# First layer's weighted expert rows: through a table in memory, or by products with the one-hot

## The chip, the cores and the metric

The kernel runs on one core of one Trainium2 chip. The metric is the time of one execution in microseconds of device time, lower is better. A core has a matrix engine (TensorE, PE in the profile; its weight loads are PEld), VectorE (DVE), ScalarE (ACT), GpSimd (POOL) and SyncE (SP), and 16 DMA engines that serve the queues of all of them.

## What is computed

Two layers of a diffusion backbone over 256 latent and 256 context tokens of width 1024. Each layer has four mixers (gated recurrence, short convolution, retention, attention), an output projection and a mixture of experts. In the first layer the experts serve all 512 tokens, in the second only the 256 latent ones. The part that matters here:

```python
def hierarchical_moe(h, w_rg, b_rg, w_re, b_re, w_gate, w_up, w_down):
    # top-1 of 4 expert groups, then top-2 of the 4 experts in it
    ...
    combine = jnp.sum(one_hot(expert_id, N_EXPERTS) * weights[..., None], axis=1)
    y = jnp.zeros(h.shape, jnp.float32)
    for e in range(N_EXPERTS):                       # 16 experts
        hidden = silu(h @ w_gate[e]) * (h @ w_up[e]) # 1024 -> 512
        y = y + combine[:, e:e + 1] * (hidden @ w_down[e])
    return y
...
x = x + mod_x[5] * y[latent];  ctx = ctx + mod_c[5] * y[context]
```

So every token gets the weighted sum of two expert rows, and that sum goes to the residual X, times a gate per column.

## The kernel before

X is kept transposed: for each of 8 column blocks j a tile of 128 columns (partitions) by 256 tokens, for latent and context tokens (`X(j, s)`).

The experts are worked through by token slots. Every expert has 64 or 96 slots, in blocks of 32; a *round* is 128 slots, four blocks. The first layer has 10 rounds (`rounds`, from `BLOCKS[0] = (2, 3, 3, 2)`), the second has 8. A round that holds two experts uses two column groups of 64 in TensorE; one that has blocks of three slots to an expert uses four of 32. All expert products are in float32.

For the first layer, the code traces each round r as follows (loop in `moe`): `gate_up(r)` multiplies the slots' rows with the gate and up weights (tiles `g` and `u`) and forms `hs`; `fetch(r + 2)` computes slots and weights of a later round and issues the gather of its rows from the memory copy `hd` on POOL's queue; `place(r + 1)` transposes the gathered rows (`gx`); `turned(hs)` transposes the hidden values (`hT`); `down(r, hT)` multiplies with the down weights (`d`, two PSUM buffers).

Expert weights arrive in tiles of 1 MB on SP's queue, in the order of use, as many in flight as `keep(LIVE[l][...])` says. All large tiles, weights, gathered rows and outputs, share 22 slabs (`NSLAB`). One-hots and hidden values share the six tiles of tag "t".

What becomes of a round's output differs. In rounds 0 to 7 of the first layer (`r < by_dma`) `down` scales it by the slot's weight, half on ACT and half on VectorE, and an indirect DMA on POOL's queue writes the rows to a table `ys` in memory, with two rows for every token; the row number is computed in `weigh` (lines from 1368 on), from a fourth plane of `mw_` that tells first from second expert. The table was filled with zeros earlier, in the first layer's mixers (line 992). After round 7, `collect` reads the table back, adds the two rows of each token and, in round 9, transposes them (32 transposes, line 1525) and adds them to X.

Rounds 8 and 9, and all rounds of the second layer, go the other way: `down` splits the weighted output into a high and a low float32r half (`ohl`, VectorE and ACT), `mark` writes a one-hot of the round's slots by tokens (`P`), and `scatter` multiplies both halves with it: per column block j, two rounds by two halves are 4 products (tile `sct`, 512 columns in the first layer, 256 in the second), which VectorE then adds to X times the gate (line 1501, two instructions in the first layer). `scatter` is a generator; one step is one column block. Its PSUM buffers are named by tags: `TGS = (("a",), ("a", "pj"))` for the two layers, while the last pair gets `TG[1]`, "pj" with three buffers. There is one buffer "a".

The order of instructions on each engine is made when the kernel is built: earlier traced ones first, a later one moved up where an earlier one is expected to wait. `tc.issue_after(x)` keeps instructions behind x.

Of the kernel before, what the change touches and what calls it, by code (L numbers as in the profile page):

```python
# [63 lines left out]
SF = ('pf', 1, 7)  # L64
NTT = 6

LIVE = [[5, 6, 4, 7, 14, 14, 15, 11, 8], [5, 5, 8, 11, 15, 18, 12]]

SPLIT = [['VG', 'VV', 'VG', 'VG', 'VG', 'VG', 'VG', 'VG', 'VV', 'VG', 'VG', 'VG', 'VG', 'VG'], ['VG', 'VG', 'VG', 'VG', 'VG', 'VG', 'VG', 'VG', 'VG', 'VG', 'VG', 'VG', 'VG', 'GV']]

# [45 lines left out]
def build(tc, xT, cT, vec, cst, ada, w_in, w_out, wg, wu, wd, outT, es, dbg=None):  # L116
# [20 lines left out]
    def ps(tag, shape=(512,), name="ps"):  # L137
        return psp.tile([128] + list(shape), F32, name=nm(name), tag=tag, bufs=PSB[tag])
# [18 lines left out]
    def tt(out, a, b, op, eng=V):  # L157
        return eng.tensor_tensor(out, a, b, op=op)  # L158
# [305 lines left out]
    def mixers(l, X, sums, first, fill, deep):  # L464
# [522 lines left out]
                pre[g] = split_w(take('in', l, g), ENG[l][g])  # L987
        weave((chain(hgrn_out(), att_norm()), MW[l][2]), (chain(ret_v(), conv()), MW[l][3]), (decays(), MW[l][4]), (fill(1), MW[l][5]))
        keep(deep[1])
        if full:  # L990
            zero = wt([512], "t")
            G.memset(zero, 0.0)
            for i in range(4):
                nc.scalar.dma_start(ys[256 * i:256 * i + 256].rearrange("(p a) (b f) -> p (a b) f", a=2, b=2),
                                    zero[:, None, :].to_broadcast([128, 4, 512]))
        for g in PST[l][1]:
            if g not in pre:
                pre[g] = split_w(take('in', l, g), ENG[l][g])
# [115 lines left out]

    keep_ = [con.tile([128, 4, 16], F32, name=k) for k in ("posm", "ovc")]
    mb_ = con.tile([128, 4, 16], BF16, name="mb")
    mw_ = con.tile([128, 4, 4, 16], BF16, name="mw")

    ys = drm.tile([2 * NT + 128, 1024], F32, name="ys")

    def moe(l, X, sums, gate, filler):
        n = NT if l == 0 else NX
# [200 lines left out]
        if sorted_:  # L1323
            by_load(comb16)

        mw = mw_[:, :nch, 0:3]
        NP = 3
        if not direct:

            NP = 4  # L1330
            r16, f16 = e_.rearrange("p c g e -> p c (g e)"), rest.rearrange("p c g e -> p c (g e)")
            V.tensor_scalar(rest, sets(rank)[:, :, 1:5], 1.0, None, op0=OP.is_equal)
            tt(rest, rest, mb4, OP.mult)
            if sorted_:
                by_load(f16)
            V.tensor_copy(mw_[:, :nch, 3], f16)
        V.tensor_copy(mw[:, :, 0], comb16)
        tt(rest16, comb16, mw[:, :, 0], OP.subtract)
        V.tensor_copy(mw[:, :, 1], rest16)
# [8 lines left out]
        V.tensor_copy(flag, pf[0:1, 0:1])  # L1348
        NR = len(rounds)

        by_dma, ysl, yrow, behind = 0 if direct else NR - 2, {}, [], [None]

        def weigh(q, Sq):

            nb = nbs[q]
            for r_ in range(nb):
                p = ps("m", [NP, 4], name="ww")
                for c in range(nch):
                    mm(p, Sq[:, c, 128 * r_:128 * r_ + 128], mw_[:, c, 0:NP, 4 * q:4 * q + 4], c == 0, c == nch - 1)
                w = wt([1], "wsl", bufs=6)  # L1360
                jk = wt([4, 4], "wslj", bufs=2)
                eo = C_EXP + (0 if nb == 3 else 12) + 4 * r_
                tt(jk[:, 0:NP], p, late(eo, 4)[:, None, :].to_broadcast([128, NP, 4]), OP.mult)
                V.tensor_reduce(w, jk[:, 0:3], axis=AX.XY, op=OP.add)
                ws[base[q] + r_] = w
                if base[q] + r_ < by_dma:

                    fx = idxf[base[q] + r_]
                    y, yi = wt([3], "ysl", bufs=2), wt([1], "ysi", I32, bufs=6)
                    V.tensor_reduce(y[:, 0:1], jk[:, 3], axis=AX.X, op=OP.add)  # L1370
                    V.tensor_scalar(y[:, 1:2], late(C_TOK + 1, 1), float(2 * NT + 256), None, op0=OP.add)
                    V.scalar_tensor_tensor(y[:, 1:2], fx, 0.0, y[:, 1:2], op0=OP.is_lt, op1=OP.mult)
                    V.scalar_tensor_tensor(y[:, 2:3], fx, 2.0, y[:, 0:1], op0=OP.mult, op1=OP.add)
                    tt(yi, y[:, 1:2], y[:, 2:3], OP.add)
                    ysl[base[q] + r_] = yi

        def fetch(r):
            q, i = rounds[r]
# [13 lines left out]
        def place(r):  # L1392

            if direct:
                S = wt([nch * 128], "t").rearrange("p (c s) -> p c s", c=nch)
                slot_of(S.rearrange("p c (e s) -> p c e s", e=2), 2 * r, 2, cap0)
                x = rowt[(r + 1) // 2][:, r % 2].rearrange("p (j s) -> p j s", j=8)
            else:
                row = rowt.pop(r)
                x = row[:, 1].rearrange("p (j s) -> p j s", j=8)  # L1400
                rv = row[:, 0].rearrange("p (j f) -> p j f", j=8)
            for hf in range(2):
                p = ps(TG[2][hf], [4, 128], name="gx")
                for j in range(4):
                    if direct:
                        for c in range(nch):
                            mm(p[:, j], hrow[c].rearrange("p (j f) -> p j f", j=8)[:, 4 * hf + j], S[:, c], c == 0, c == nch - 1)
                    else:
                        T.transpose(p[:, j], rv[:, 4 * hf + j], ident)
                if hf:  # L1410
                    act(x[:, 4:8], p)
                else:
                    V.tensor_copy(x[:, 0:4], p)  # L1413
            Xg[r] = x
            if r >= by_dma:
                mark(r)

        def experts(r):
            q, i = rounds[r]
# [35 lines left out]
        def turned(hs):  # L1455
            p = ps(TG[3], name="hT")
            for jj in range(4):
                behind[0] = T.transpose(p[:, 128 * jj:128 * jj + 128], hs.rearrange("p (f e) -> p f e", e=4)[:, :, jj], ident)
            hT = wt([512], "t").rearrange("p (a b) -> p a b", a=4)
            act(hT, p.rearrange("p (a b) -> p a b", a=4))  # L1460
            return hT

        def down(r, hT):
            pd = [ps("h", name="d") for _ in range(2)]
            for jj in range(4):
                if jj == 2:
                    finish(r, 4)
                for nn in range(2):
                    for b, m, e in columns(r):
                        mm(pd[nn][b:b + m], hT[:, jj, b:b + m], W[e][4 + jj // 2][:, jj % 2, 512 * nn:512 * nn + 512],  # L1470
                           jj == 0, jj == 3)
            finish(r, 5)
            w = ws.pop(r)
            if r < by_dma:
                if r % 2 == 0:
                    yrow.append(sl([2, 1024], name="y"))
                o = yrow[-1][:, r % 2]
                act(o[:, 0:512], pd[0], AF.Copy, scale=w)
                V.tensor_scalar(o[:, 512:1024], pd[1], w, None, op0=OP.mult)
                nc.gpsimd.indirect_dma_start(out=ys[:, :], out_offset=bass.IndirectOffsetOnAxis(ap=ysl.pop(r), axis=0),  # L1480
                                             in_=o, in_offset=None)
                return
            ohl = sl([2, 1024], F32R, "o")
            for nn in range(2):
                fs = slice(512 * nn, 512 * nn + 512)
                act(ohl[:, 0, fs], pd[nn], AF.Copy, scale=w)
                V.scalar_tensor_tensor(ohl[:, 1, fs], pd[nn], w, ohl[:, 0, fs].bitcast(F32),  # L1487
                                       op0=OP.mult, op1=OP.subtract)
            outs[r] = ohl
# [17 lines left out]
                        outs.pop(r), Pm.pop(r)  # L1507
                yield

        def collect(tags=None):  # L1510

            tags = tags or TGS[l]
            yt = []
            for c in range(nch):
                y = sl([2, 1024], name="y")
                nc.gpsimd.dma_start(y, ys[256 * c:256 * c + 256].rearrange("(p a) f -> p a f", a=2))
                yt.append(y)
            yield
            for c in range(nch):
                tt(yt[c][:, 0], yt[c][:, 0], yt[c][:, 1], OP.add, (V, G)[c % 2])  # L1520
            for j in range(8):
                p = ps(tags[j % len(tags)], name="sct")
                for c in range(nch):
                    with tc.issue_after(behind[0].ins):
                        T.transpose(p[:, 128 * c:128 * c + 128], yt[c][:, 0, 128 * j:128 * j + 128], ident)
                for s in range(ns):
                    V.scalar_tensor_tensor(X(j, s), p[:, NX * s:NX * s + NX], gate[:, j, s:s + 1], X(j, s),
                                           op0=OP.mult, op1=OP.add)
                yield

        fetch(0)
        fetch(1)
        if not by_dma:
            mark(0)
        pend, sc = [], iter(())
        for r in range(NR):
            if r >= NR - 2 and l + 1 < DEPTH:
# [5 lines left out]
                fetch(r + 2)  # L1543
            if r + 1 < NR:
                place(r + 1)
            if by_dma:
                hs = turned(hs)
                if r == NR - 1:
                    run(sc)
            else:  # L1550
                for _ in range(SCJ[l]):
                    next(sc, None)
                hs = turned(hs)
            down(r, hs)
            if r < by_dma:
                if r == by_dma - 1:
                    sc = collect(TG[1] + TGS[l])
                    next(sc)
                continue
            pend.append(r)  # L1560
            if len(pend) == 2 and r < NR - 1:
                run(sc)
# [202 lines left out]
```

## Time and profile before

| | us |
|---|---|
| median of 3 runs | 1180.85 |
| lowest, highest | 1178.14, 1181.89 |
| profiled execution, its own time | 1176.74 |
| its span, first to last instruction | 1175.0 |

| engine | busy, us | share |
|---|---|---|
| PE | 1092.7 | 93% |
| PEld | 688.1 | 59% |
| DVE | 512.1 | 44% |
| ACT | 370.3 | 32% |
| POOL | 218.8 | 19% |

The profile is that of one execution. Engines run side by side and wait for each other by semaphores. The share of busy time is a mean over stages that differ, so the profile is read for the stage that the change touches: the first layer's experts, from about 395 to 670 us, where 96 weight tiles of 1 MB stream in. In the rows further on, "idle before" in brackets is the time an engine stood still before an instruction, and the arrow names what ended it.

### The profile page before, as it was taken

What the parts mean: (1) busy time and instruction counts of PE and PEld (TensorE: products, weight loads), DVE (VectorE), ACT (ScalarE), POOL (GpSimd) and SP (SyncE); (2) the same over time, 40 slices, a digit from 0 to 9 for tenths busy, and PEclk for the clock granted to TensorE, in tenths of its full rate; (3) what the DMA queues carried; (4) which work ended last, traced back from release to release, by engine and by line L of the source; (5) the groups of instructions that cost most, each with busy time, mean ns of one, the idle gap of its engine ahead of it and who ended that gap; (6) DMA issues with size and microseconds to landing.
All of it is one profiled execution on the core that took longest, in us unless ns stands there. A gap on an engine that the chain in (4) does not pass through costs nothing. (4 is left out here: it accounts for less than half of the span.)

```text
span 1175.0 us, 16520 instructions
## 1 busy us (share of the span) xinstructions
PE 1092.7 (93%) x6577; PEld 688.1 (59%) x6577; DVE 512.1 (44%) x1000; ACT 370.3 (32%) x628; POOL 218.8 (19%) x168
## 2 busy tenths in 40 slices
PE   5999989999999989999898889999899799999997
PEld 2699876674576453333233459867767644565653
DVE  1647576656663810101001574686876421212122
ACT  5544357533442101001010454347754211101010
POOL 0235270410131001000012323353203200000000
PEclk9999999999999999999999989999999899999999
DMA  9812105765437999999799942472255889899991
GB/s 385 327 66 68 41 1 215 261 238 218 172 120 273 416 421 422 420 421 422 306 390 409 379 180 85 178 275 73 102 185 179 323 323 420 359 423 420 422 388 37
DMA packets 48548, 316.18 MB, mean 269 GB/s; under 512 B 5712, under 2 KB 7376, under 8 KB 12112
## 3 DMA queue, kind: packets, MB, share of 16 engines
q1 hardware_dynamic: 42320, 295.52, 63.4%
q0 software_dynamic: 3024, 13.11, 2.7%
q10 hardware_dynamic: 3120, 6.41, 1.5%
q8 instruction: 55, 0.90, 0.3%
q14 instruction: 29, 0.24, 0.1%
HBM read 303.49 MB, written 11.53 MB: 268 GB/s over the span
## 5 line engine op out<-in xcount | busy, mean ns | idle before, releaser
L152 PE MATMUL pf<-hxh,wsp 128*128 128x512 f32 (+1 forms) x640 | 178.9, 363 | 11.0 <-ACT hxh L155 5.0
L152 PE MATMUL g<-w,row 128*64 128x512 f32 (+1 forms) x704 | 148.0, 598 | 2.3 <-DVE row L1413 2.1
L152 PE MATMUL u<-w,row 128*64 128x512 f32 (+1 forms) x704 | 142.6, 593 | 1.3 <-DMA w<-in_wu_dram 1.3
L158 POOL TENSOR_TENSOR wsp<-w,wsp 128x1024 fp32r<-128x1024 f32 x34 | 94.2, 2774 | 250.9 <-ACT wsp L155 204.9
L152 PE MATMUL d<-w,t 128*64 128x512 f32 (+1 forms) x704 | 133.3, 597 | 1.5 <-ACT t L155 1.4
L152 PEld LDWEIGHTS pf<-hxh,wsp 128*128 128x128 f32 x640 | 114.5, 191 | 34.4 <-ACT hxh L155 7.1
L152 PE MATMUL pf<-hxl,wsp 128*128 128x512 f32 (+1 forms) x320 | 114.7, 360 | 2.2 <-POOL hxl L158 2.0
L158 DVE TENSOR_TENSOR t<-t,u 128x512 f32<-128x512 f32 x18 | 12.4, 687 | 232.6 <-PE u L152 232.6
L152 PEld LDWEIGHTS u<-w,row 128*64 128x64 f32 (+1 forms) x704 | 55.3, 127 | 74.9 <-issue 69.5
L152 PEld LDWEIGHTS g<-w,row 128*64 128x64 f32 (+1 forms) x704 | 52.7, 127 | 76.2 <-issue 68.6
L152 PEld LDWEIGHTS d<-w,t 128*64 128x64 f32 (+1 forms) x704 | 48.0, 128 | 78.5 <-issue 67.7
L152 PE MATMUL ptk<-wsp,hxh 128*128 128x256 f32 x480 | 90.3, 287 | 0.0
L155 ACT ACTIVATE wsp<-w 128x1024 fp32r<-128x1024 f32 x72 | 73.7, 1053 | 13.9 <-PE pf L152 7.7
L152 PEld LDWEIGHTS ptk<-wsp,hxh 128*128 128x128 f32 x480 | 75.2, 191 | 2.3 <-issue 1.2
L152 PE MATMUL pw<-mixh,wsp 128*128 128x512 f32 (+1 forms) x256 | 68.5, 352 | 2.2 <-POOL wsp L158 1.3
L158 POOL TENSOR_TENSOR K<-K,F 64x512 f32<-64x512 f32 (+1 forms) x46 | 58.6, 1273 | 59.4 <-issue 24.1
L152 PEld LDWEIGHTS pf<-hxl,wsp 128*128 128x128 f32 x320 | 61.5, 192 | 12.7 <-POOL hxl L158 3.4
L152 PE MATMUL ptk<-wsp,hxl 128*128 128x256 f32 x240 | 68.2, 284 | 0.0
L158 DVE TENSOR_TENSOR wsp<-w,wsp 128x1024 fp32r<-128x1024 f32 x38 | 52.3, 1377 | 31.2 <-ACT wsp L155 31.1
L158 DVE TENSOR_TENSOR Q<-Q,F 64x256 f32<-64x256 f32 (+3 forms) x60 | 55.8, 935 | 22.8 <-PE sc L152 19.5
L155 ACT ACTIVATE row<-gx 128x512 f32<-128x512 f32 x18 | 10.8, 598 | 163.7 <-PE gx L152 88.6
L155 ACT ACTIVATE t<-g 128x512 f32<-128x512 f32 x18 | 10.7, 597 | 162.6 <-PE g L152 162.6
(281 smaller groups left out, 1562.5 us busy)
## 6 DMA issues: line engine op xcount, KB each, us to landing
w<-in_wg_dram SPq DMA_DIRECT2D x64, 1024.0 KB, 10.5
w<-in_wu_dram SPq DMA_DIRECT2D x64, 1024.0 KB, 12.1
w<-in_wd_dram SPq DMA_DIRECT2D x64, 1024.0 KB, 16.1
w<-in_ada_dram SPq DMA_DIRECT2D x48, 1024.0 KB, 6.7
w<-in_w_in_dram SPq DMA_DIRECT2D x28, 1024.0 KB, 7.9
w<-in_w_out_dram SPq DMA_DIRECT2D x8, 1024.0 KB, 6.1
X<-in_xT_dram SPq DMA_DIRECT2D x4, 1024.0 KB, 5.1
ys<-t ACTq DMA_DIRECT2D x4, 1024.0 KB, 5.9
```

The source lines that it names most:

```text
L152: return T.matmul(out, lhsT, rhs, start=start, stop=stop, **kw)
L155: return S.activation(out, in_, f, **kw)
L158: return eng.tensor_tensor(out, a, b, op=op)
```

## The change

The table `ys`, its zero fill, the row numbers in `weigh`, the fourth plane of `mw_`, the indirect writes and `collect` go. All ten rounds of the first layer end as rounds 8 and 9 did: high and low half, one-hot, and products, always for two rounds together. The steps of a pair's `scatter` are traced in the rounds after it: `SCJ[0] = 6` column blocks in the next round, between `place` and `turned`, and the last two in the round after that. The last pair (8, 9) stays where it was. The weight tiles in flight from round 1 on go from 15 to 13, and from round 8 on from 11 to 12. The second layer's code stays as it is.

```diff
-LIVE = [[5, 6, 4, 7, 14, 14, 15, 11, 8], [5, 5, 8, 11, 15, 18, 12]]
+LIVE = [[5, 6, 4, 7, 14, 14, 13, 12, 8], [5, 5, 8, 11, 15, 18, 12]]
...
-        if full:
-            zero = wt([512], "t")
-            G.memset(zero, 0.0)
-            for i in range(4):
-                nc.scalar.dma_start(ys[256 * i:256 * i + 256].rearrange("(p a) (b f) -> p (a b) f", a=2, b=2),
-                                    zero[:, None, :].to_broadcast([128, 4, 512]))
...
-    mw_ = con.tile([128, 4, 4, 16], BF16, name="mw")
-
-    ys = drm.tile([2 * NT + 128, 1024], F32, name="ys")
+    mw_ = con.tile([128, 4, 3, 16], BF16, name="mw")
...
-        mw = mw_[:, :nch, 0:3]
-        NP = 3
-        if not direct:
-
-            NP = 4
-            r16, f16 = e_.rearrange("p c g e -> p c (g e)"), rest.rearrange("p c g e -> p c (g e)")
-            V.tensor_scalar(rest, sets(rank)[:, :, 1:5], 1.0, None, op0=OP.is_equal)
-            tt(rest, rest, mb4, OP.mult)
-            if sorted_:
-                by_load(f16)
-            V.tensor_copy(mw_[:, :nch, 3], f16)
+        mw = mw_[:, :nch]
...
-                if base[q] + r_ < by_dma:
-
-                    fx = idxf[base[q] + r_]
-                    y, yi = wt([3], "ysl", bufs=2), wt([1], "ysi", I32, bufs=6)
...
-                    ysl[base[q] + r_] = yi
...
-            if r >= by_dma:
-                mark(r)
+            mark(r)
...
-            if r < by_dma:
-                if r % 2 == 0:
-                    yrow.append(sl([2, 1024], name="y"))
-                o = yrow[-1][:, r % 2]
-                act(o[:, 0:512], pd[0], AF.Copy, scale=w)
-                V.tensor_scalar(o[:, 512:1024], pd[1], w, None, op0=OP.mult)
-                nc.gpsimd.indirect_dma_start(out=ys[:, :], out_offset=bass.IndirectOffsetOnAxis(ap=ysl.pop(r), axis=0),
-                                             in_=o, in_offset=None)
-                return
...
-        def collect(tags=None):
...
-            if by_dma:
-                hs = turned(hs)
-                if r == NR - 1:
-                    run(sc)
-            else:
-                for _ in range(SCJ[l]):
-                    next(sc, None)
-                hs = turned(hs)
-            down(r, hs)
-            if r < by_dma:
-                if r == by_dma - 1:
-                    sc = collect(TG[1] + TGS[l])
-                    next(sc)
-                continue
+            for _ in range(SCJ[l]):
+                next(sc, None)
+            down(r, turned(hs))
             pend.append(r)
             if len(pend) == 2 and r < NR - 1:
                 run(sc)
```

## Rows read from the trace of the kernel before

**Rows 1.** Busy time in stretches: length, busy us (instructions), PEclk, DMA share, GB/s.

```profile
core 0: us, PE busy (x) PEld busy (x) DVE busy (x) ACT busy (x) POOL busy (x), PEclk, DMA share, GB/s
400.00:500.00 100.00, 92.84 (x554) 39.14 (x552) 19.88 (x87) 9.01 (x15) 7.00 (x7) 0.97 1.01 421
500.00:600.00 100.00, 95.14 (x704) 32.55 (x704) 9.43 (x21) 9.70 (x16) 7.79 (x8) 0.98 0.95 385
...
570.00:580.00 10.00, 9.65 (x40) 3.41 (x40) 1.08 (x2) 1.20 (x2) 0.00 (x0) 0.83 0.42 143
220.00:230.00 10.00, 10.00 (x51) 7.42 (x50) 4.18 (x5) 7.07 (x13) 1.27 (x4) 1.00 0.84 307
```

**Rows 2.** PE in order of time: start, us, instruction, rounds 4 and 8.

```profile
517.01 1.07 PE L1409 MATMUL gx<-cb,row 128*128 128x128 f32 x8
518.48 0.75 PE L1458 MATMUL hT<-cb,t 128*128 128x128 f32 x4 [0.40 <-DVE row L1413]
...
519.98 7.09 PE L152 MATMUL d<-w,t 128*32 128x512 f32 x64
...
622.42 7.09 PE L152 MATMUL d<-w,t 128*64 128x512 f32 x32 [0.75 <-ACT t L155]
```

**Rows 3.** PE's waits from 390 to 672 us: total us, times, longest.

```profile
PE gx L1409 <- DMA row<-hd,ixi: 6.4, 2, 3.3
PE hT L1458 <- DVE row L1413: 3.3, 8, 0.4
PE ww L152 <- DVE ixa L1289: 1.5, 2, 1.1
PE d L152 <- ACT t L155: 1.4, 2, 0.7
PE u L152 <- DMA w<-in_wu_dram: 1.3, 1, 1.3
PE sct L152 <- DVE X L1501: 0.9, 1, 0.9
PE hT L1458 <- DVE t L158: 0.8, 1, 0.8
```

**Rows 4.** Groups by shape, 390 to 672 us: count, busy us, mean ns, idle before.

```profile
L152 PE MATMUL sct<-t,o 128*128 128x512 f32 x32 | 8.2, 403 | 0.9 <-DVE X L1501 0.9
...
L1525 PE MATMUL sct<-cb,y 128*128 128x128 f32 x32 | 4.3, 278 | 0.0
```

**Rows 5.** PE in order of time, round 9: collect's transposes and the down products.

```profile
647.01 2.35 PE L1525 MATMUL sct<-cb,y 128*128 128x128 f32 x20
649.29 1.93 PE L152 MATMUL d<-w,t 128*64 128x512 f32 x6
651.15 0.66 PE L1525 MATMUL sct<-cb,y 128*128 128x128 f32 x4
...
660.22 3.07 PE L152 MATMUL sct<-t,o 128*128 128x512 f32 x12
```

**Rows 6.** PE in order of time, round 6.

```profile
569.76 1.09 PE L1409 MATMUL gx<-cb,row 128*128 128x128 f32 x8 [3.06 <-DMA row<-hd,ixi]
...
574.00 7.51 PE L152 MATMUL d<-w,t 128*64 128x512 f32 x32
```

**Rows 7.** POOL in order of time, around rounds 5 and 6.

```profile
557.70 0.98 POOL L1480 DMA_INDIRECT ys<-y,ysi  x1 [9.19 <-DMA ys<-y,ysi]
558.98 0.98 POOL L1301 DMA_INDIRECT row<-hd,ixi  x1 [0.30 <-DMA w<-in_wd_dram]
```

**Rows 8.** POOL in order of time, the first gather.

```profile
404.41 1.16 POOL L1301 DMA_INDIRECT row<-hd,ixi  x1 [22.99 <-DVE mw L1341]
```

**Rows 9.** DVE in order of time, additions of the last pair of products.

```profile
663.14 4.01 DVE L1501 SCALAR_TENSOR_TENSOR X<-sct,mods,X 128x256 f32<-128x256 f32 x10
```

**Rows 10.** The page's DMA queues: packets, MB, share of 16 engines.

```profile
q0 software_dynamic: 3024, 13.11, 2.7%
```

**Rows 11.** PE in order of time, second layer's round 2.

```profile
1015.56 0.74 PE L152 MATMUL sct<-t,o 128*128 128x256 f32 x4 [0.58 <-DVE X L1501]
```

More of the change, by code (lines that the diff above doesn't have):

```diff
@@ L1349, in moe @@
         NR = len(rounds)
-        by_dma, ysl, yrow, behind = 0 if direct else NR - 2, {}, [], [None]
         def weigh(q, Sq):
@@ L1356, in weigh @@
             for r_ in range(nb):
-                p = ps("m", [NP, 4], name="ww")
+                p = ps("m", [3, 4], name="ww")
                 for c in range(nch):
-                    mm(p, Sq[:, c, 128 * r_:128 * r_ + 128], mw_[:, c, 0:NP, 4 * q:4 * q + 4], c == 0, c == nch - 1)
+                    mm(p, Sq[:, c, 128 * r_:128 * r_ + 128], mw_[:, c, :, 4 * q:4 * q + 4], c == 0, c == nch - 1)
                 w = wt([1], "wsl", bufs=6)
-                jk = wt([4, 4], "wslj", bufs=2)
+                jk = wt([3, 4], "wslj", bufs=2)
                 eo = C_EXP + (0 if nb == 3 else 12) + 4 * r_
-                tt(jk[:, 0:NP], p, late(eo, 4)[:, None, :].to_broadcast([128, NP, 4]), OP.mult)
-                V.tensor_reduce(w, jk[:, 0:3], axis=AX.XY, op=OP.add)
+                tt(jk, p, late(eo, 4)[:, None, :].to_broadcast([128, 3, 4]), OP.mult)
+                V.tensor_reduce(w, jk, axis=AX.XY, op=OP.add)
                 ws[base[q] + r_] = w
-                if base[q] + r_ < by_dma:
-                    fx = idxf[base[q] + r_]
-                    y, yi = wt([3], "ysl", bufs=2), wt([1], "ysi", I32, bufs=6)
[L1370 to L1374, printed above, removed]
-                    ysl[base[q] + r_] = yi
         def fetch(r):
@@ L1457, in turned @@
             for jj in range(4):
-                behind[0] = T.transpose(p[:, 128 * jj:128 * jj + 128], hs.rearrange("p (f e) -> p f e", e=4)[:, :, jj], ident)
+                T.transpose(p[:, 128 * jj:128 * jj + 128], hs.rearrange("p (f e) -> p f e", e=4)[:, :, jj], ident)
             hT = wt([512], "t").rearrange("p (a b) -> p a b", a=4)
@@ L1508, in scatter @@
                 yield
-        def collect(tags=None):
[L1512 to L1529, printed above, removed]
         fetch(0)
         fetch(1)
-        if not by_dma:
-            mark(0)
+        mark(0)
         pend, sc = [], iter(())
```

## The prediction

> **What bounds the kernel now.** The views were read in this order: busy time in stretches, the order of TensorE's instructions in one round, TensorE's waits in the expert stage, and then the rows of the operations that come and go.
>
> The change works on the first layer's expert stage, about 395 to 670 us. There two resources are nearly full at once [rows 1]: the DMA engines are at a share of 1.01 and 421 GB/s, and PE is busy for 92.8 and 95.1 us of two stretches of 100. Which of them sets the pace? The reader is to look at 570 to 580 us: the DMA share falls to 0.42 (143 GB/s) while PE is busy for 9.65 of 10 us. The transfers had run ahead and were waiting for buffers, and PE went on. [Rows 2] say the same from PE's side: the down products of a round take 7.09 us at 520 us, as 64 narrow ones, and 7.09 us at 622 us, as 32 of twice the width. A step waiting for data would not repeat to the hundredth. And [rows 3]: of PE's waits from 390 to 672 us only 1.3 us are for a weight transfer (a row of 0.2 us more is not shown); all its waits make 16.0 us, with 0.4 us in two rows that are not shown. So PE sets the pace, the DMA engines run close behind, and what is added on PE costs its own time less what it fills of those 16 us.
>
> **The change, part by part.**
>
> *Products added.* Rounds 0 to 7, which went to the table, now form four pairs, each of 8 column blocks x 2 rounds x 2 halves (high and low part) = 32 products of 512 columns. Before has exactly one such pair, rounds 8 and 9: 32 products, busy 8.2 us [rows 4], that is 0.256 us each. Four pairs: 4 x 8.2 = **+32.8 us**.
>
> *What it costs to put them between others.* In before the pair runs at the end, in runs of up to 12. The new ones run inside rounds, and layer 0's tag list has one PSUM buffer for them ("a"): block j+1 waits until VectorE has added block j to X. The last round shows what the instruction order does with such waits: the transposes of the collected rows stand ahead of the down products in the code, and in the trace one bank's 4 transposes alternate with 6 and more down products [rows 5]. So a block goes into the down products whenever its buffer is free. That breaks column groups which otherwise run side by side: 6 down products took 651.15 - 649.29 = 1.86 us, where 7.09 / 32 x 6 = 1.33 us is the undisturbed pace [rows 2, 5]. Over the whole step: 660.22 - 647.01 = 13.2 us, less 7.1 for the down products and 4.3 for the transposes [rows 4], leaves 1.8 us for three breaks, 0.6 us each. Per pair I count five breaks: of the six blocks issued in the even round one fills the wait before the hidden transposes (hT), one the wait for their copy, four fall into the down products; of the two in the odd round one breaks something. 4 x 5 x 0.6 = **+12.0 us**. The lower end is 0 (all blocks in waits or at group edges). The upper end is the case that they don't interleave, rival B.
>
> The Trainium skill, "TensorEngine Tiling (Array Packing)", section Key Properties, states that changing the tiling mode drains TensorE, and these breaks go from column tiles to the full array and back. By that rule the term cannot be nothing; without it the sum below would be 12.0 us smaller. The 1.8 us for three breaks agree with it.
>
> *Collect removed.* In round 9 the time from the first transpose to the first product of the last pair is 13.2 us, in which the down products need 7.1 us and the wait for the copy of hT about 0.9 (0.7 as the wait for it in [rows 3], and 0.2 on the way). The rest, **-5.3 us**, goes. The reads of the table and the two additions on POOL lay beside.
>
> *Waits that go, or are filled.* (1) Round 6's place step waited 3.06 us for its gathered rows [rows 6]. The gather was issued at 558.98, behind a table write that itself stood 9.19 us on POOL's queue until the previous table write had landed [rows 7]. With no table write there, the gather no longer stands behind it. PE then ran at a granted clock of 0.83, between its levels of 2.4 and 1.2 GHz [rows 1]: from the place step to the end of the down products 574.00 + 7.51 - 569.76 = 11.8 us, against 519.98 + 7.09 - 517.01 = 10.1 in an undisturbed round [rows 2, 6]. 3.1 + 1.7 = -4.8. (2) hT waits for VectorE's copy in 8 rounds, 3.3 us [rows 3]; in 7 of them a block of products is now ready: -2.9. (3) The same work covers one wait of 1.1 (ww), one of 0.7 (d) and one of 0.8 (hT for its input) [rows 3]: -2.6. (4) The wait of 1.3 for weights: transfers get a lead: -1.3. (5) The first gather's wait, 3.3 us: the gather was issued after the VectorE copy of line 1341 [rows 8], and VectorE has a few steps fewer ahead of it. Between 0 and -3.3; I take -1.0, since the rows' write to memory may have come last. Sum: **-12.6 us**.
>
> *At nothing.* VectorE gets 16 additions of 0.40 us per pair [rows 9], a second output step and a mark per round, and loses the additions from collected rows, the slot arithmetic (line 1368 on) and a fourth plane of weights; it is busy for 9.4 us of 100 in 500 to 600, and ACT for 9.7 [rows 1]. PE's products cover this; where an addition stands ahead of the SwiGLU product on VectorE's queue, hT and PE wait up to 0.8 us for it, some 3 us over four pairs, which stays in the range. POOL loses eight table writes and two additions and has only gathers left. The zero fill (4 MB, issued by ACT's queue at 224 to 233 us) ran where PE was busy for 10.00 of 10.00 us [rows 1]; nothing waited for it. The 8.4 MB of table writes and reads, of the queue's 13.11 MB [rows 10], return 8.4 / 0.421 = 20 us of DMA time that PE does not need. The weights in flight fall from 15 to 13 tiles of 1 MB, each consumed in about 2.5 us: still some 25 us ahead.
>
> *Sum.* 32.8 + 12.0 - 5.3 - 12.6 = **+26.9 us**. On the profiled execution (1176.74 us, span 1175.0) that is 1203.6. That run lies 4.1 us below the median of the three others, 1180.85, on which the sum gives 1207.8. I forecast **1207.5**. My own range for it, with 0 to 1.3 for the first gather's extra, 3 us of VectorE's and half to one and a half of the breaks, is 1196 to 1220.
>
> **The rivals.**
>
> *B: the blocks wait for their buffer instead of interleaving.* In the second layer's rounds a block on one buffer came 0.58 us after the last, waiting for VectorE's X, and the hidden transposes came only afterwards [rows 11]. There a block is half as wide. Here one turn is 4 products (3 x 0.256 + 0.40 = 1.2 us, by the mean in [rows 4]), two additions (0.8 us, [rows 9]) and a handoff of about 0.1: 2.1 us. 32 x 2.1 = 67 instead of 44.8: +49 us, 1230. It decides if hT or the down products are not ready when a block waits. Against it: [rows 5]. Chance 0.16.
>
> *C: the transfers set the pace after all.* Then the 20 us of DMA time come back, and the products fall into time in which PE would wait for weights: 1180.85 - 20 = 1161. It decides where a round's weights take longer than PE's work. For it: 421 GB/s and 1.01 over 100 us [rows 1]. Against: 0.42 at 570 to 580, and 1.3 us of waits. Chance 0.04. The Trainium skill, "DMA: Bandwidth & Descriptors", section Specifications, gives a fabric ceiling of 435 GB/s; 421 is 97% of that, so by the page the engines have nothing to spare. It would speak for this rival, but the 1.3 us of waits do not bear it out.
>
> *D: the products settle into waits and edges.* No breaks, every wait of [rows 3] filled and the slow clock gone: 32.8 - 5.3 - 16.0 - 1.7 = +9.8, 1191 (range 1187 to 1196). For it: a round has waits where a block fits. Against: they are 0.4 us, a block is 1.0. Chance 0.20.
>
> *E: two weight tiles fewer ahead.* If a gather or output tile then holds back the loads, each round's start could wait two tiles, 5 us: up to 8 x 5 = 40 on top, 1247. Chance 0.04.
>
> *F: nothing gets done differently* (the blocks are moved where nothing waits for them): within 0.3%. The floor of +9.8 speaks against it: PE has no more to give. Chance 0.01.
>
> **How the numbers follow.** Forecast 0.55, D 0.20, B 0.16, C 0.04, E 0.04, F 0.01. The predicted time is the forecast's. Leaving out the upper part of B, E, C and F gives 1188 to 1234. A measurement of this kernel can tell about 0.3% from no change; slower by more than that are the forecast, D but for its edge, B and E: 0.93; faster 0.04 (C); within 0.03.
>
> **What would show it.** Right: in the changed kernel's expert stage 160 products of 512 columns of about 0.25 us; PE busy share unchanged or higher, DMA share well under 1.0; groups of 4 products between down products, whose step takes 9 us and more in even rounds instead of 7.1; no wait for gathered rows in round 6; rounds some 3 us longer each. B shows as waits for X on PE of about 1 us, some 20 of them. D shows as down products still at 7.1 us. Wrong: waits for weights in PE's list (E), or rounds no longer than before (C).

## The result, and the profile after

The changed kernel takes 1199.99 us (median of 4 runs, 1197.67 to 1202.04) against 1179.49 of the kernel before: a ratio of 1.0173, interval 1.0157 to 1.0189, so 20.5 us slower. The forecast was 1207.5 within 1188 to 1234, slower. The profiled execution has a span of 1195.8 us, 20.8 more than before; the ledger below goes by the spans.

The expert stage first, in the columns of [rows 1].

```profile
400.00:500.00 100.00, 96.34 (x570) 41.06 (x571) 26.04 (x73) 9.54 (x16) 4.87 (x5) 1.00 0.96 393
500.00:600.00 100.00, 99.54 (x653) 37.78 (x655) 26.82 (x58) 12.07 (x19) 3.74 (x4) 1.00 0.83 307
```

PE went from 95.1 to 99.5 us of the second hundred, and the DMA share from 0.95 to 0.83: PE sets the pace, and the DMA engines, which no longer carry the table, have time left. VectorE went from 9.4 to 26.8 and is still far from full.

PE's waits from 390 to 695 us in the changed kernel, as in [rows 3] (the window is longer because the stage is):

```profile
PE ssb L152 <- PEq L1499: 2.4, 1, 2.4
PE sct L152 <- DVE X L1461: 1.8, 1, 1.8
PE g L152 <- DMA w<-in_wg_dram: 1.1, 1, 1.1
PE hT L1427 <- ACT row L155: 0.9, 2, 0.7
PE hT L1427 <- DVE row L1383: 0.9, 2, 0.5
...
```

The two waits for gathered rows (6.4 us before) are gone, and the waits for hT's inputs fell from 4.1 to 1.8 us. The wait for weights has only moved: 1.3 us in round 9 of before, 1.1 us now, at the gate products of round 2. The first row lies behind the stage and is not in the list of before, which ended ahead of it.

The groups that grew, as in [rows 4]:

```profile
L152 PE MATMUL d<-w,t 128*64 128x512 f32 x192 | 47.3, 600 | 0.0
L152 PE MATMUL sct<-t,o 128*128 128x512 f32 x160 | 47.1, 418 | 1.9 <-DVE X L1461 1.8
...
L152 PE MATMUL d<-w,t 128*32 128x512 f32 x256 | 31.6, 597 | 0.0
```

And PE in order of time in round 4, to be read against [rows 2], where the same 64 down products ran in one piece of 7.09 us:

```profile
523.67 1.09 PE L1379 MATMUL gx<-cb,row 128*128 128x128 f32 x8
524.51 1.18 PE L152 MATMUL sct<-t,o 128*128 128x512 f32 x4
525.53 0.64 PE L1427 MATMUL hT<-cb,t 128*128 128x128 f32 x4
...
527.07 1.20 PE L152 MATMUL sct<-t,o 128*128 128x512 f32 x4
528.20 1.91 PE L152 MATMUL d<-w,t 128*32 128x512 f32 x10
530.03 1.20 PE L152 MATMUL sct<-t,o 128*128 128x512 f32 x4
531.17 1.92 PE L152 MATMUL d<-w,t 128*32 128x512 f32 x16
533.02 1.20 PE L152 MATMUL sct<-t,o 128*128 128x512 f32 x4
```

This is the order that the prediction described: the first block fills the place of the wait for hT, the second comes while hT is copied, the others go into the down products one at a time, as the one buffer comes free.

### The profile page after: what moved, and what is told of

Its sections match the earlier page's. It is cut to its first block, busy times and chain, and to the rows that moved or that the text cites. A ratio compares the mean times of both kernels' runs of the same rounds, so it can differ in the third digit from the quotient of the medians.

```text
span 1195.8 us, 16722 instructions
## 1 busy us (share of the span) xinstructions
PE 1124.5 (94%) x6673; PEld 706.0 (59%) x6673; DVE 535.3 (45%) x1017; ACT 375.4 (31%) x636; POOL 203.4 (17%) x153
## 5 line engine op out<-in xcount | busy, mean ns | idle before, releaser
L152 PE MATMUL pf<-hxh,wsp 128*128 128x512 f32 (+1 forms) x640 | 179.6, 365 | 11.4 <-ACT hxh L155 5.5
L152 PE MATMUL d<-w,t 128*64 128x512 f32 (+1 forms) x704 | 138.0, 597 | 0.0
L1461 DVE SCALAR_TENSOR_TENSOR X<-sct,mods,X 128x256 f32<-128x256 f32 x112 | 49.7, 480 | 63.0 <-PE sct L152 62.6
L1447 DVE SCALAR_TENSOR_TENSOR o<-d,wsl,o 128x512 fp32r<-128x512 f32 x36 | 26.3, 748 | 106.9 <-ACT o L155 106.0
L152 PE MATMUL sct<-t,o 128*128 128x512 f32 (+1 forms) x288 | 67.5, 364 | 5.7 <-DVE X L1461 5.3
## 6 DMA issues: line engine op xcount, KB each, us to landing
w<-in_wu_dram SPq DMA_DIRECT2D x64, 1024.0 KB, 10.6
```

Of the source, the lines that this page charges most:

```text
L152: return T.matmul(out, lhsT, rhs, start=start, stop=stop, **kw)
```

## The experiments

Theory P is the prediction's: PE sets the pace, the products cost their time on PE, and the blocks on one buffer break the column groups of the other products. Rival D in the texts below is the prediction's rival C (the transfers set the pace). All kernels were run beside the kernel before.

To see where the time went, four traces are cut at the same two points of PE's order: from the first down product of round 0 to the first product of the last pair that follows round 9's down products. (2 to 4 products of the last pair run ahead of that point in the kernels without the table.) In the columns of [rows 1]: before, whose end is in [rows 5], then the changed kernel without the early products, with two buffers (both below), and as it is.

```profile
418.25:660.22 241.97, 230.44 (x1453) 86.06 (x1451) 31.88 (x81) 22.43 (x37) 21.51 (x21) 0.99 0.98 402
...
416.90:648.28 231.38, 221.99 (x1423) 79.17 (x1421) 29.55 (x62) 26.85 (x45) 6.97 (x7) 0.99 0.99 408
...
416.92:668.96 252.04, 250.56 (x1551) 106.21 (x1550) 56.72 (x126) 27.41 (x45) 6.57 (x7) 1.00 0.93 375
...
416.80:680.11 263.31, 260.52 (x1552) 103.20 (x1551) 57.12 (x126) 27.60 (x45) 6.56 (x7) 1.00 0.91 361
```

| kernel | stage, us | PE idle, us | step |
|---|---|---|---|
| before | 242.0 | 11.5 | |
| changed, no early products | 231.4 | 9.4 | -10.6: table, collect and their waits go |
| changed, two buffers | 252.0 | 1.5 | +20.7: products, in runs |
| changed | 263.3 | 2.8 | +11.3: one buffer, products in fours |

The spans differ by 20.8 us: 21.3 in this stage, less 1.5 gained ahead of it (418.25 to 416.80, see the first gather below), and 0.9 behind it.

**Without the early products.** The products of rounds 0 to 7 and their additions are left out.

```diff
-                sc, pend = scatter(pend), []
+                sc, pend = iter(()) if l == 0 else scatter(pend), []
```

> The changed kernel without the 128 products of rounds 0 to 7 and their additions to X (that part of the experts' sum is left out); outputs, one-hots and the last pair stay. Theory P: the products cost their whole time on PE, 128 x 0.256 = 32.8 us and 6 us of breaks, less the 1 to 2 us of waits that they fill: 37 us less than the changed kernel, about 1163 us, ratio to before 0.986. Rival D: with the products gone the weight transfers set the pace, 96 tiles at 2.49 us, so that PE shows 10 us or more of waits for weights and the time falls by 25 us or less, 1175 us or more.

Measured: 1168.51 us, ratio 0.9912 (0.9896 to 0.9929); by the ratios (1.0173 - 0.9912) x 1179 = 30.8 us less than the changed kernel. Theory P expected 37, rival D at most 25. No wait for weights is in PE's list of the stage, so the transfers don't set the pace even with nothing added. That it is 31 and not 37 has its main reason in the waits that come back, in the stage from 417 to 648 us:

```profile
PE hT L1427 <- DVE row L1383: 2.5, 6, 0.5
PE d L152 <- DVE o L1447: 2.1, 1, 2.1
PE sct L152 <- ACT o L155: 1.3, 1, 1.3
PE hT L1427 <- DVE t L158: 0.9, 1, 0.9
...
PE hT L1427 <- DVE t L1359: 0.7, 1, 0.7
...
```

With the rows not shown they sum to 9.4 us. Three of them, the two for the output o and that for line 1359 (a one-hot), 4.1 us, appear neither in before nor in the changed kernel. The rest of the reason is the clock: ahead of this window the first gathered rows were late again (2.0 us), and after that wait PE ran at 0.91 for 23 us, where the changed kernel has 1.00; that is about 23 x 0.09 = 2.1 us.

```profile
417.00:440.00 23.00, 23.00 (x99) 9.12 (x98) 0.12 (x1) 0.60 (x1) 0.94 (x1) 0.91 1.01 426
```

**Two buffers for the blocks.** The tag "pj" beside "a", as in the second layer.

```diff
-TGS = (("a",), ("a", "pj"))
+TGS = (("a", "pj"), ("a", "pj"))
```

> The changed kernel with a second PSUM tag for the blocks of the first layer ("a" and "pj" in place of "a" alone), so that blocks come two and more in a row and break the down products less often. Theory P with breaks of about 0.2 us per block: half of the breaks go, 3 us less, 1197 us. By the prediction's own 0.6 us for each of 20 breaks: 6 us less, 1194 us. Rival: the gate and up products lose a buffer of "pj" and wait: 1202 us or more.

Measured: 1188.12 us, ratio 1.0076 (1.0053 to 1.0098); by the ratios (1.0173 - 1.0076) x 1179 = 11.4 us less than the changed kernel. I had expected 3 or, by the prediction's own price, 6, taking it that half the breaks stay. Nearly none stays, in round 4:

```profile
520.72 1.09 PE L1379 MATMUL gx<-cb,row 128*128 128x128 f32 x8
521.57 5.65 PE L152 MATMUL sct<-t,o 128*128 128x512 f32 x22
527.05 0.64 PE L1427 MATMUL hT<-cb,t 128*128 128x128 f32 x4
...
528.44 7.09 PE L152 MATMUL d<-w,t 128*32 128x512 f32 x64
```

The blocks run through ahead of hT, and the down products are back at 7.09 us. The groups say the same for the stage: products 42.7 us busy in place of 47.1, down products 42.8 and 28.3 in place of 47.3 and 31.6, together 12.2 us less.

```profile
L152 PE MATMUL d<-w,t 128*64 128x512 f32 x192 | 42.8, 595 | 0.1
L152 PE MATMUL sct<-t,o 128*128 128x512 f32 x160 | 42.7, 408 | 1.8 <-DVE X L1461 1.5
...
L152 PE MATMUL d<-w,t 128*32 128x512 f32 x256 | 28.3, 594 | 0.0
```

The rival (gate and up products missing a "pj" buffer) falls: no wait of the kind appears.

**Blocks kept ahead of hT.** One buffer, but hT is held behind the last block traced before it.

```diff
+                spread["W"] = spread[j]
...
+            spread.pop("W", None)
...
-            down(r, turned(hs))
+            with tc.issue_after(spread["W"].ins) if l == 0 and "W" in spread else nullcontext():
+                hT = turned(hs)
+            down(r, hT)
```

(`spread["W"]` is the last product of the block traced last.)

> The changed kernel with hT kept behind the last block of products traced before it, so that the blocks can't go into the down products and wait for their one buffer instead. It prices rival B of the prediction, which set one turn of the buffer at 2.1 us against 1.03 us of products. By that price: 32 blocks x (2.1 - 1.2) = 28 us more than the changed kernel, less what later rounds' gate products fill: 1215 to 1228 us, ratio to before 1.030 to 1.041. If the buffer's turn is hidden by other products anyway (rival): the breaks in the down products go and the time is the changed kernel's or 6 us less, 1194 to 1200 us.

Measured: 1206.15 us, ratio 1.0240 (1.0220 to 1.0259): 0.0067 x 1179 = 8 us more than the changed kernel, less than the 15 to 28 expected and not the gain of the rival. The trace shows why: where a block may not go into the down products, it goes into the next round's gate and up products, and only a few waits for the buffer are left, four of 4.2 us in all.

```profile
PE sct L152 <- DVE X L1462: 4.2, 4, 1.1
```

In order of time, round 4 of the same kernel:

```profile
527.90 1.20 PE L152 MATMUL sct<-t,o 128*128 128x512 f32 x4
529.04 1.05 PE L152 MATMUL u<-w,row 128*32 128x512 f32 x4
530.17 1.17 PE L152 MATMUL sct<-t,o 128*128 128x512 f32 x4
532.40 1.17 PE L152 MATMUL sct<-t,o 128*128 128x512 f32 x4 [1.06 <-DVE X L1462]
```

The last two rows are the price that rival B was given: one turn of the buffer, 532.40 - 530.17 = 2.23 us, against 2.1 forecast. The price was right; what the rival missed is that other work is put into the gap when the order is made, as the kernel is built.

**Before without the table writes.** The eight indirect writes are left out; collect reads the zeros, so the experts' sum of rounds 0 to 7 is missing.

```diff
-                nc.gpsimd.indirect_dma_start(out=ys[:, :], out_offset=bass.IndirectOffsetOnAxis(ap=ysl.pop(r), axis=0),
-                                             in_=o, in_offset=None)
```

> The kernel before without the eight indirect table writes (collect reads the zero fill; the experts' sum of rounds 0 to 7 is left out of the result). Theory P (PE sets the pace): only the wait for gathered rows in round 6 and the slow clock behind it go, 4.8 us by the trace of before: ratio to before 0.996, about 1175 us, and the DMA share falls without PE's weight waits changing. Rival D (the transfers set the pace): 4.2 MB at 421 GB/s come back, 10 us and more: ratio 0.991 or less, about 1169 us.

Measured: 1171.66 us, ratio 0.995 (0.993 to 0.997), 5.9 us. That is theory P's 4.8 us and not the 10 of the rival. The order on POOL: the gather of round 7's rows was issued at 537.29, some 28 us before they were used, where [rows 7] had 558.98; its wait and the slow clock in round 6 are gone.

```profile
537.29 0.94 POOL L1301 DMA_INDIRECT row<-hd,ixi  x1 [23.29 <-DMA w<-in_wu_dram]
```

and PE's place step of round 6, without a wait:

```profile
565.83 1.09 PE L1409 MATMUL gx<-cb,row 128*128 128x128 f32 x8
```

One thing the expectation had otherwise: PE's waits for weights did change. Here PE came to the gate products of round 2 earlier, because the first gather cost it no wait, and stood there for 3.21 us. Before:

```profile
451.10 6.62 PE L152 MATMUL g<-w,row 128*32 128x512 f32 x57 [0.21 <-DMA w<-in_wg_dram]
```

Without the writes:

```profile
451.84 6.62 PE L152 MATMUL g<-w,row 128*32 128x512 f32 x57 [3.21 <-DMA w<-in_wg_dram]
```

The changed kernel waits there for 1.07 us, until 451.73. So at this one point the transfers do set the pace, and what PE gains ahead of it is lost. It is not the table's traffic: the weights come no earlier without the writes.

**Before with the changed kernel's tiles in flight.**

```diff
-LIVE = [[5, 6, 4, 7, 14, 14, 15, 11, 8], [5, 5, 8, 11, 15, 18, 12]]
+LIVE = [[5, 6, 4, 7, 14, 14, 13, 12, 8], [5, 5, 8, 11, 15, 18, 12]]
```

> The kernel before with the changed kernel's weight tiles in flight (13 and 12). It tests what released the gather of round 7, for which PE waited 3.06 us in before: if it was a free slab, two more free slabs let it go earlier, the wait and the slow clock go, 1175 us, ratio 0.996. If it was the table write ahead of it on POOL's queue, the wait stays: ratio 1.000.

Measured: 1173.41 us, ratio 0.9942 (0.9925 to 0.9959): faster than both kernels. The wait for gathered rows is gone from PE's list. But the reading "a free slab or the table write" was too simple, as POOL's order shows:

```profile
544.48 0.98 POOL L1480 DMA_INDIRECT ys<-y,ysi  x1 [32.20 <-ACT t L155]
554.46 0.98 POOL L1480 DMA_INDIRECT ys<-y,ysi  x1 [9.00 <-DMA ys<-y,ysi]
555.74 0.98 POOL L1301 DMA_INDIRECT row<-hd,ixi  x1 [0.30 <-issue]
```

The gather still stands behind two table writes, the second 9 us behind the first. Only the first went 3 us earlier, 544.48 in place of 547.52, and that was enough. What moved it is in the traces: VectorE's half of that round's output. Before:

```profile
546.00 0.75 DVE L1479 TENSOR_SCALAR y<-d,wsl 128x512 f32<-128x512 f32 x1
```

With 13 tiles:

```profile
542.96 0.74 DVE L1479 TENSOR_SCALAR y<-d,wsl 128x512 f32<-128x512 f32 x1
```

Both it and the write are 3.04 us earlier. In before the slot arithmetic of a later round, which waits for PE, stands ahead of it on VectorE from 545.20 on; with 13 tiles that arithmetic comes at 566.44. So the table write ahead of the gather held it, as the second reading said, and it went earlier because VectorE's order, made when the kernel is built, came out otherwise. That the edit of the tiles led to that order is all these runs show of its part. Some of what the change gave back on waits was to be had with the table in place.

**Tiles in flight back to 15 and 11, in the changed kernel.** The edit is the reverse of the last one.

> The changed kernel with the weight tiles in flight as they were (15 from round 1 on, 11 from round 8 on, in place of 13 and 12). Theory P: PE does not wait for weights with 13, so nothing changes: 1200 us within 0.2%, unless output rows or gathers no longer find a slab. Rival E of the prediction (the shorter lead costs): faster by the 1.1 us weight wait of the changed kernel or more, 1199 us or less.

Measured: 1202.73 us, ratio 1.0207 (1.0190 to 1.0224), against 1.0173 (1.0157 to 1.0189): not faster, if anything slower. The prediction's rival E (a shorter lead costs) falls.

**Zero fill kept.** The fill of the table, which nobody reads then, is put back into the changed kernel's mixers.

> The changed kernel with the zero fill kept (4 MB of writes in the mixers to a table that nobody reads). Theory P: it ran beside a full PE and costs nothing: 1200 us within 0.2%. Rival: those writes delay weights or ACT's queue in the mixers: 1202 to 1206 us.

Measured: 1198.11 us, ratio 1.0162 (1.0137 to 1.0188): no difference from the changed kernel. That edit is worth nothing, as predicted.

**Fourth plane kept.** It is computed and not used.

> The changed kernel with the fourth plane of weights computed again and not used: about 2.5 us more on VectorE ahead of the copy to the planes. It tests why the first gather's wait is gone. If VectorE released the first gather, the gather is 2 to 3 us later and PE waits for its rows again: 1202 to 1203 us, with a wait for the gathered rows in round 0 of 2 to 3 us. If the write of the rows to memory released it: 1200 us, no such wait.

Measured: 1201.39 us, ratio 1.0181 (1.0158 to 1.0204): no difference that can be told. A wait for the rows came back in round 0, 2.3 us, which by the text above speaks for VectorE. The traces say otherwise. The address of the gather was ready earlier than in the changed kernel, not later (VectorE's line 1285 at 400.15 us, not 402.50), and yet the gather went at 404.12. What differs among the kernels is the granted clock ahead of the stage, and with it when PE gets there:

| kernel | granted clock, 380 to 390 us | address ready | first gather | first place step | its wait for rows, us |
|---|---|---|---|---|---|
| before | 1.00 | 400.30 | 404.41 | 414.55 | 3.34 |
| fourth plane kept | 1.00 | 400.15 | 404.12 | 413.39 | 2.33 |
| changed, no early products | 1.00 | 400.42 | 403.99 | 413.32 | 1.99 |
| blocks ahead of hT | 1.00 | 400.29 | 403.94 | 413.15 | 1.96 |
| changed, 15 tiles | 0.95 | 401.29 | 402.30 | 412.36 | none |
| before, no writes | 0.92 | 401.82 | 402.83 | 413.06 | none |
| zero fill kept | 0.92 | 401.40 | 402.41 | 412.56 | none |
| changed | 0.90 | 402.50 | 403.51 | 413.57 | none |
| changed, two buffers | 0.88 | 402.63 | 403.63 | 413.70 | none |
| before, 13 tiles | 0.75 | 403.59 | 404.60 | 414.69 | none |

Where TensorE runs slower at 380 to 390 us, it comes later and finds its rows. Both groups hold kernels with the table and without it; three of the ten are the kernel before up to there, and among them alone the clock goes from 1.00 to 0.75. So the gain on this wait and the loss on the clock belong together, and these runs show no part of the change in it.

The table also shows what releases the gather. In the six kernels below full clock it follows the address by 1.00 or 1.01 us. In the four others it goes 3.6 to 4.1 us after the address; there the last write of the rows to memory comes last. Before:

```profile
L1147 ACTq DMA_DIRECT2D hd<-hrow x1: 326/326/326, 389.9 to 389.9; - x1
...
DMA to landing us min/median/max: 13.5/13.5/13.5
```

It landed at 389.9 + 13.5 = 403.4 us, 1.0 ahead of the gather in [rows 8]. In the changed kernel the writes issued from 389.7 to 392.1 took 9.1 to 9.7 us and had landed by 401.8, ahead of the address. Why the last one took 13.0 to 13.5 us in the four kernels at full clock is open.

## Why the prediction was right

**The bound.** Right, but for one point. PE set the pace, the transfers did not: without the table writes 5.9 us come back and not 10, without products there is no wait for weights, and in the changed kernel the DMA share falls to 0.83. The point is about 451 us, where seven of the ten kernels wait 0.2 to 3.2 us for round 2's gate weights.

**Products, +32.8.** Nearly right. In a run of 22 they take 5.48 / 22 = 0.249 us each (521.57 to 527.05 above), 31.9 us for 128.

**Breaks, +12.0.** Right in sum: 11.3 us by the stage, 11.4 by the ratios, between two kernels that differ in the buffer alone. Of the 11.3, 10.0 are PE's busy time (260.52 - 250.56) and 1.3 are waits that the second buffer fills. The single price was 0.6 us for 20 breaks; the trace has 22 blocks with column products on both sides, one of which stays with two buffers: 10.0 / 21 = 0.48 us each. It is not spread evenly. The first break in a step is dear: in round 4, 10 down products took 530.03 - 528.20 = 1.83 us where 7.09 / 64 x 10 is 1.11. The following 16 took 1.85 where 1.77 is the pace.

The trace agrees with the drain rule that the prediction took from the Trainium skill ("TensorEngine Tiling (Array Packing)", Key Properties): no block in between was free; a block of four takes 531.17 - 530.03 = 1.14 us between down products, against 4 x 0.249 = 1.00 in a run.

**Table and collect, -5.3; round 6's gather, -4.8; weights, -1.3.** Together -11.4; removing all of it without adding products gave -10.6. Right in sum, and in part by luck: the kernel without products has the 4.1 us of waits and the 2.1 us of slow clock of its own (above), and on the other side a slow stretch of before goes that the prediction overlooked. From 490 to 500 us before had a granted clock of 0.83, as in [rows 1]'s 570 to 580, about 10 x 0.17 = 1.7 us. Before, in the columns of [rows 1]:

```profile
490.00:500.00 10.00, 8.77 (x42) 3.45 (x43) 4.07 (x27) 1.19 (x2) 0.99 (x1) 0.83 1.01 420
```

Without products:

```profile
490.00:500.00 10.00, 9.15 (x48) 3.76 (x46) 2.24 (x8) 1.24 (x3) 1.35 (x1) 1.00 1.01 423
```

The changed kernel has 1.00 there too, and so have both other kernels with the table, without writes and with 13 tiles, so it was not the products that raised it.

The reason given for the gather, the table write ahead of it on POOL's queue, stands: without writes it goes 21.7 us earlier. That it needed their removal does not: with 13 tiles it came in time behind them. The wait for weights did not go: 1.5 us in the list of before, 1.1 in the changed kernel's.

**Waits filled by products, -5.5 (items 2 and 3).** The products in runs cost 20.7 us of stage for 31.9 us of work, so 11.2 us of them cost nothing. That is not a miss of 5.7 us, though. 7.9 of the 11.2 are idle time (9.4 to 1.5 us), and 4.1 of these are waits that the kernel without products has and before does not. Another 2.1 are the slow clock of that kernel. Before and the changed kernel compared directly, PE's idle time in the stage goes from 11.5 to 2.8 us, by 8.7; the prediction took 9.9 out of it (3.1 of item 1, these 5.5, and 1.3 for weights). So the waits were sized about right.

**The 6 us between the forecast's +26.9 and the 20.8 of the spans.** For the stage the prediction makes 27.9 us (26.9, with the 1.0 of the first gather, which lies ahead of it); 21.3 were measured. Mis-sized were the breaks, by 2.0, the products, by 0.9, and the slow clock of before, by the 1.7 of 490 to 500 us; the waits go 1.2 us the other way. That makes 3.4 of the 6.6 us; the rest these traces do not assign.

**First gather, -1.0.** PE was 1.5 us earlier at the start of the stage, but not for the reason given: no shorter work on VectorE, but the clock ahead of the stage. The doubt that the prediction added, that the rows' write to memory may have come last, was right for before. And the gain was not kept: after its wait for weights at 451 us the changed kernel was 0.6 us behind before (451.73, 451.10).

**The rivals.** B's price per turn was right (2.23 us against 2.1; its 0.1 for the handoff stood in no row, and the trace has 0.04 and 0.15 us around additions of 0.87), its place wrong: the blocks were interleaved. C, E and F fell. D, products that settle into waits without breaks, is what the kernel with two buffers is: +9 us, forecast as +9.8.

## What to carry to other kernels

Before work is moved from DMA to TensorE, look which of the two waits for the other: a DMA share of 1.01 beside a full PE is no bound by itself, and only the moment in which one of them lets go tells (here 570 to 580 us). When products are put between column-tiled ones, give them a second PSUM buffer, so that they run in one piece; here that was 11 us of 20. And a buffer count tuned for one form of a kernel is worth trying alone in the other: 13 in place of 15 tiles made the kernel before 0.6% faster, though the wait that went with it went by another order of instructions and not by the buffers themselves.

## What the runs showed of the hardware that was not expected

After the first break into a step of column-tiled products the next ones are cheap: 10 products in 1.83 us, then 16 in 1.85 each time. The column groups seem to go on shifted against each other and still run side by side; that is argued from these times, and was not tried by itself.

The granted clock differed in the same stretch, 380 to 390 us, from 1.00 to 0.75 between kernels, 1.00, 0.92 and 0.75 among the three whose code is the same up to there. It was worth up to some 3 us (PE ready for the first place step at 411.2 in before, at 414.7 with 13 tiles), which a wait for rows mostly took back.
